# New order keys for every stage of a hybrid diffusion step on one NeuronCore

## The chip, the cores and the metric

The kernel runs on one core of one Trainium2 chip. The metric is the device time of one execution in microseconds (us). Before the change it is 1241.89 us, the median of three runs (1240.9 to 1245.12).

The engines are called by their names in the profile: PE is TensorE (matmuls; PEld is its weight load), DVE is VectorE, ACT is ScalarE, POOL is GpSimd, and SP is SyncE, which here only issues DMAs.

## The reference

One inference step of a backbone with two layers, on 256 context tokens and 1024 latent tokens of width 1024. The first layer is a gated linear attention (GLA) in both directions, the second a softmax attention with 8 query heads and 2 key heads. Each layer normalises its input, modulates it by a conditioning vector, runs its mixer, multiplies the result by a SiLU gate, projects it and adds it to the input. Cut to what matters:

```
for l in range(2):
    mod_p, mod_s = silu(c_ctx) @ w_ada[l] + b_ada[l], silu(c) @ w_ada[l] + b_ada[l]
    hp = rms_norm(xp, g[l]) * (1 + sc_p) + sh_p          # context tokens
    hs = rms_norm(xs, g[l]) * (1 + sc_s) + sh_s          # latent tokens
    if l == 0:                                            # GLA, 4 heads, chunks of 64
        q, k, v, gate = split(h @ w_in)
        decay = log_sigmoid((h @ wa1[d]) @ wa2[d] + ba[d]) / 16
        o = scan_forward(q, k, v, decay) + scan_backward(q, k, v, decay)
        out = (rms_norm(o) * silu(gate)) @ w_out
    else:                                                 # attention
        q, k = rope(rms_norm(q)), rope(rms_norm(k))       # rope on latent tokens alone
        out = (softmax(q k^T / sqrt(128)) v * silu(gate)) @ w_out
    x = x + gt * out
```

The outputs are both token streams, the final scan states of the context, and the keys and values of the context.

## The kernel before

Tokens come in ten tiles of 128 (two of context, eight latent). Every matmul of a projection is done in three parts of half precision: an operand is scaled by a power of two and split into a high and a low part (names ending in hi and lo, or h and l), and PE adds hi x hi, hi x lo and lo x hi (line 247). Making the low part is an operation of DVE with two inputs in SBUF, such as L1382, L309, L330 or L566. Transposes of half-precision tiles are DMAs that SP issues (L1383 for the softmax, L1055 for the rows of the first output projection).

The stages, with the times at which they run in the profile:

- Start (to about 84 us): weights of the modulation are loaded and multiplied, then the tokens are normalised (L535 to L542), transposed by PE (L548) and modulated. In one form of a modulation ACT makes the high part and DVE the full value (L561, L562), in the other ACT makes the full value and POOL copies the high part (L564, L565); DVE makes the low part (L566). Between the groups of tokens the small weights of the decay (the "rank") are split (L601 to L616) and its scales are worked out (L623 to L635).
- GLA layer (84 to about 480 us): head by head, tile by tile, a slot each. In a slot run the decay (L733 to L748), the decayed queries and keys (L758 to L768), the part within a chunk (intra, L781 to L793), the scan's outer products and states (L805 to L834; POOL does L830), the local part, the combination of both directions (L865 to L872), values and gates (L714, L718), the SiLU (L351 to L362) and the gated output (L879, L881), which SP stores in HBM (L882).
- Between the layers (480 to about 700 us): a fifth round over the tiles finishes the last head while the first output projection starts; rows are loaded again, split (out_prep, L1049 to L1055), projected with the residual (L1019 to L1030), modulated for the second layer (L508 to L520), and the first keys and queries are made (L1161 to L1207; POOL does the rotation L1172 and the square roots L238).
- Attention (700 to about 1147 us): ten steps of two query tiles and four heads. In each, scores (L1344) go to PSUM, DVE takes their maximum (L1347), ACT the exponential (L1352). A second piece, rest, normalises them: the high part by POOL for the first tile (L1379) or by ACT for the second (L1381), the low part by DVE (L1382), then the transposing DMA. The values of two heads back are multiplied by the transposed weights (L247, PT and vh), gated (L1407) and stored through POOL's queue (L1408). Key tiles of the context are written out through POOL's queue too (L1293, L1296). In the last step the rows of the first output tiles are loaded and prepared, and two pieces of the output (z.out, L1558 to L1562) and the last values (z.val) end it.
- Output (1147 us to the end): the second output projection, tile by tile (y, L247), with no order keys of its own.

The order of the instructions on each engine is fixed when the program is built. The framework keeps a running number that rises by one with each traced instruction, and its scheduler plays the program through a timeline and gives each engine, whenever it is free, the ready instruction with the lowest number. A step's number can be shifted:

```
def later(self, name, i=""):
    n = LATER.get(f"{name}{i}", LATER.get(name, 0))
    self.tc.cur_priority += n
    yield
    self.tc.cur_priority -= n
```

A negative entry of the table LATER lets the step go ahead of as many instructions, a positive one puts it behind them, among what is ready. A second argument picks one place: "a9.s1.3" is the second score of the fourth head in the last attention step, where "a9.s1" holds for the others. An explicit issue_after still holds an instruction behind another one on its engine. In attention, the names are a0 for the first two heads, a9 for the last step and a for the rest; s0 and s1 are the scores of the two tiles, q and qr the next query, val the values, key a key tile, gate the gates, rest the normalisation. In the GLA layer, gated, silu, A, ks, u, o, combine and the like are the parts of a slot, with a 9 for the fifth round; wo2, wo3, eres and emod belong to the weights and the early tiles of the first output projection. Names with x. belong to the stage between the layers, and those with s. to the start: s.rk is the rank's weights and scales, s.n1 and s.n2 the normalising of the second and third group of tokens, s.v the first value weights, s.q0 and s.q1 the first queries and keys.

## Time and profile before

| | value |
|---|---|
| median of three runs | 1241.89 us |
| the three runs | 1240.9, 1241.89, 1245.12 us |
| span of the profiled execution | 1240.9 us |
| instructions | 22365 |
| PE busy | 96% of the span |
| DVE busy | 76% |
| ACT busy | 55% |
| POOL busy | 26% |

The page gives, for the profiled execution, only its span, from the first to the last instruction; no time of its own is given beside it. A busy engine is one that has an instruction under way. Matmuls overlap: one of 256 columns is shown for 273 ns, though the next follows 109 ns later. PEclk is the share of full clock that PE was granted. A wait is put down to the operation that ended it, and a line may be that of a helper that many steps share, so a group is told apart by its tile names.

### The profile page before, as it was taken

The page shows a single profiled execution, that of the slowest core. Times are in us where ns is not written, and L with a number is a line of the kernel's source. Part 1 is how long each engine was busy: PE and PEld are TensorE (multiplying, and loading weights), DVE is VectorE, ACT ScalarE, POOL GpSimd, SP SyncE. Part 2 cuts the span into 40 slices and gives each one's busy share as a digit, 9 for nine tenths or more (in the row PEclk, how much of TensorE's full clock was granted, in tenths as well). Part 3 has the DMA queues.
Part 4 walks back from the last instruction along what each step waited for, and adds up shares of the span by engine and source line. Part 5 has one row for each costly group of instructions (what it writes and reads, how often), then busy time and mean ns, then how long its engine had stood idle before and what let it go on. Part 6 is the DMA issues. An engine that isn't in the chain of part 4 may idle for free. (4 is left out here: it accounts for less than half of the span.)

```text
span 1240.9 us, 22365 instructions
## 1 busy us (share of the span) xinstructions
PE 1190.7 (96%) x7990; PEld 778.3 (63%) x7990; DVE 944.9 (76%) x2177; ACT 687.0 (55%) x1694; POOL 320.5 (26%) x566
## 2 busy tenths in 40 slices
PE   5799999999999999799999999999999999989998
PEld 3467765655556566667776666776767666666444
DVE  4787779887888789976875787877767587786653
ACT  2565556665666657742333576666767676664110
POOL 0132122323321143311212443431322343311000
PEclk9999999999999999999999999999999999999999
DMA  9511566456555544489978787777958666979432
GB/s 378 196 69 73 196 202 228 127 185 203 175 191 164 189 132 161 112 186 307 204 174 203 178 163 138 132 145 133 199 124 161 124 118 132 205 139 246 158 137 85
DMA packets 318496, 210.14 MB, mean 169 GB/s; under 512 B 257158, under 2 KB 294702, under 8 KB 310064
## 3 DMA queue, kind: packets, MB, share of 16 engines
q1 hardware_dynamic: 311232, 191.18, 60.1%
q10 hardware_dynamic: 4688, 10.57, 2.2%
q0 software_dynamic: 2464, 6.95, 2.0%
q8 instruction: 63, 1.03, 0.3%
q14 instruction: 49, 0.40, 0.1%
HBM read 108.35 MB, written 38.96 MB: 119 GB/s over the span
## 5 line engine op out<-in xcount | busy, mean ns | idle before, releaser
L247 PEld LDWEIGHTS <-hT_hi 128*128 128x128 f16 x1920 | 187.6, 98 | 122.0 <-issue 5.6
L247 PE MATMUL mm<-whi,hT_hi 128*128 128x512 f16 (+1 forms) x576 | 200.2, 348 | 3.5 <-ACT gx L718 3.0
L247 PE MATMUL mm<-whi,hT_lo 128*128 128x512 f16 (+1 forms) x576 | 200.4, 348 | 0.0
L247 PE MATMUL mm<-wlo,hT_hi 128*128 128x512 f16 (+1 forms) x560 | 194.3, 347 | 0.7 <-DVE wlo L309 0.7
L247 PEld LDWEIGHTS <-whi 128*128 128x128 f16 x1232 | 120.3, 98 | 62.1 <-issue 2.2
L1344 PE MATMUL S<-kT,wst 128*128 128x512 f16 (+1 forms) x624 | 142.1, 341 | 4.1 <-ACT p L1352 4.0
L247 PE MATMUL mm<-hT_hi,whi 128*128 128x256 f16 (+1 forms) x480 | 141.1, 294 | 2.0 <-ACT gx L1392 2.0
L247 PE MATMUL mm<-hT_hi,wlo 128*128 128x256 f16 (+1 forms) x480 | 141.1, 294 | 0.0
L247 PE MATMUL mm<-hT_lo,whi 128*128 128x256 f16 (+1 forms) x480 | 141.1, 294 | 0.0
L1382 DVE SCALAR_TENSOR_TENSOR phl<-p,srec,phl 128x1280 f16<-128x1280 f32 (+1 forms) x79 | 105.3, 1332 | 40.6 <-ACT phl L1381 26.9
L247 PEld LDWEIGHTS <-hT_lo 128*128 128x128 f16 x960 | 94.1, 98 | 61.8 <-issue 1.1
L247 PE MATMUL mm<-PT,vh 128*128 128x256 f16 x672 | 114.6, 273 | 8.1 <-DMA PT<-phl 7.8
L1347 DVE TENSOR_REDUCE smx<-S 128x1 f32<-128x1280 f32 (+1 forms) x80 | 101.3, 1271 | 27.0 <-PE S L1344 26.9
L1352 ACT ACTIVATE p<-S,snb,acol 128x1280 f32<-128x1280 f32 (+1 forms) x80 | 99.1, 1239 | 12.5 <-DVE phl L1382 7.0
L1344 PEld LDWEIGHTS <-wst 128*128 128x128 f16 x624 | 61.4, 98 | 55.7 <-issue 6.9
L247 PE MATMUL mm<-PT,vl 128*128 128x256 f16 x336 | 91.6, 273 | 0.0
L1379 POOL TENSOR_SCALAR phl<-p,srec 128x1280 f16<-128x1280 f32 (+1 forms) x40 | 53.1, 1327 | 105.0 <-DVE srec L1370 57.1
L247 PEld LDWEIGHTS <-wlo 128*128 128x128 f16 x616 | 60.2, 98 | 29.2
L247 PEld LDWEIGHTS <-vh 128*128 128x128 f16 x672 | 65.1, 98 | 18.3 <-DMA PT<-phl 7.2
L1172 POOL TENSOR_TENSOR rope<-hx,ropet 128x64 f32<-128x64 f32 x160 | 51.2, 350 | 81.3 <-ACT hx L1308 63.8
L270 DVE TENSOR_REDUCE wmx<-wst 128x1 f32<-128x512 f32 x104 | 65.1, 677 | 3.5 <-DMA wst<-in_att_w 2.0
L238 POOL TENSOR_TENSOR hrs<-hrsa,mhalf 128x2 f32<-128x2 f32 x50 | 38.7, 775 | 106.8 <-DVE hrsa L236 106.5
(383 smaller groups left out, 2684.9 us busy)
## 6 DMA issues: line engine op xcount, KB each, us to landing
wada<-in_w_ada SPq DMA_DIRECT2D x16, 1024.0 KB, 5.4
wst<-in_att_w SPq DMA_DIRECT2D x14, 1024.0 KB, 5.3
wst<-in_gla_w_in SPq DMA_DIRECT2D x12, 1024.0 KB, 5.5
og_d<-og POOLq DMA_DIRECT2D x40, 128.0 KB, 2.8
wst<-og_d SPq DMA_DIRECT2D x5, 1024.0 KB, 6.0
og_d<-gx SPq DMA_DIRECT2D x37, 128.0 KB, 2.1
xr<-x_d SPq DMA_DIRECT2D x9, 512.0 KB, 3.3
out<-xr ACTq DMA_DIRECT2D x17, 256.0 KB, 2.0
```

Of the source, the lines that this page charges most:

```text
L238: nc.gpsimd.tensor_tensor(r, a, self.mhalf[:, 0:w], ALU.pow)
L247: self.pe = self.nc.tensor.matmul(out, a, b, start=k == 0 and j == 0, stop=k == n - 1 and j == 2).ins
L270: nc.vector.tensor_reduce(mx[:, j : j + 1], st[:, 2 * j : 2 * j + 2, :], AX.XY, ALU.max, apply_absolute_value=True)
L1172: nc.gpsimd.tensor_tensor(tv[:, h, :, w, :], xv[:, h, :, 1 - w, :], sn[:, :, w, :], ALU.mult)
L1344: nc.tensor.matmul(S[:, a : a + n], x, y, start=m == 0, stop=m == 2)
L1347: last = nc.vector.tensor_reduce(mx, S, AX.X, ALU.max).ins
L1352: nc.scalar.activation(p, S, AF.Exp, scale=self.sexp, bias=nb, accum_out=den)
L1379: nc.gpsimd.tensor_scalar(hi, p, r, 2.0 ** 14, ALU.mult, ALU.mult)
L1382: nc.vector.scalar_tensor_tensor(lo, p, r2, hi, ALU.mult, ALU.subtract)
```

## The change

The table LATER keeps its 93 names; 73 of the values are set anew, 38 lower and 35 higher, by a median of 55. Nothing else in the program changes: the same instructions run on the same engines with the same operands. The entries that moved by 100 or more, and some others:

```diff
-    "A": -110,            +    "A": -375,
-    "ks": -90,            +    "ks": 10,
-    "gated": 50,          +    "gated": -20,
-    "silu": -150,         +    "silu": -395,
-    "combine9": 70,       +    "combine9": 280,
-    "eres": 110,          +    "eres": 45,
-    "wo2": 30,            +    "wo2": 185,
-    "wo3": 245,           +    "wo3": 180,
-    "x.prep": -150,       +    "x.prep": 20,
-    "x.mod": -60,         +    "x.mod": -200,
-    "x.kset": -30,        +    "x.kset": 170,
-    "x.key8": 150,        +    "x.key8": -55,
-    "s.rk": 70,           +    "s.rk": -135,
-    "s.n1": -100,         +    "s.n1": 0,
-    "s.n2": -55,          +    "s.n2": -490,
-    "s.q1": 60,           +    "s.q1": 185,
-    "s.s0": -140,         +    "s.s0": 45,
-    "s.r1": 115,          +    "s.r1": 300,
-    "s.v": 400,           +    "s.v": 580,
-    "a0.qr": 15,          +    "a0.qr": 145,
-    "a0.gate": 65,        +    "a0.gate": 130,
-    "a0.s1": 390,         +    "a0.s1": 340,
-    "a.rest.0": 100,      +    "a.rest.0": -35,
-    "a.s0.1": -15,        +    "a.s0.1": -55,
-    "a.s1.0": 55,         +    "a.s1.0": -30,
-    "a9.s1": -160,        +    "a9.s1": -60,
-    "a9.val.1": -5,       +    "a9.val.1": -105,
-    "a9.val.3": -80,      +    "a9.val.3": -265,
-    "a9.q.2": 30,         +    "a9.q.2": -120,
-    "a9.gate.2": 85,      +    "a9.gate.2": 255,
-    "a9.s1.3": -150,      +    "a9.s1.3": 185,
-    "z.val": 35,          +    "z.val": 205,
-    "z.val.0": -100,      +    "z.val.0": 55,
-    "z.val.1": 165,       +    "z.val.1": -25,
```

The old value stands on the left of each line and the new one on the right.

## The prediction

> **What bounds the kernel now.** I read the page's busy row first, then a table of windows cut where the stages change, then who TensorE (PE) waits for.

> ```profile
> span 1240.9 us, 22365 instructions
> PE 1190.7 (96%) x7990; PEld 778.3 (63%) x7990; DVE 944.9 (76%) x2177; ACT 687.0 (55%) x1694; POOL 320.5 (26%) x566
> ```

> ```profile
> core 0: us, PE busy (x) PEld busy (x) DVE busy (x) ACT busy (x) POOL busy (x), PEclk, DMA share, GB/s
> 0.00:38.00 38.00, 21.27 (x202) 13.43 (x203) 16.51 (x46) 9.67 (x18) 2.95 (x8) 1.00 0.95 365
> 38.00:84.00 46.00, 39.17 (x241) 20.42 (x240) 39.63 (x86) 30.17 (x50) 9.92 (x15) 1.00 0.29 111
> 84.00:480.00 396.00, 395.70 (x2468) 244.90 (x2467) 328.78 (x891) 243.74 (x636) 113.36 (x207) 1.00 0.52 168
> 480.00:560.00 80.00, 71.97 (x513) 52.95 (x512) 68.53 (x193) 47.85 (x121) 20.93 (x34) 0.98 0.63 169
> 560.00:700.00 140.00, 140.00 (x1039) 101.40 (x1037) 103.58 (x224) 50.92 (x134) 33.34 (x73) 1.00 0.89 216
> 700.00:745.00 45.00, 40.65 (x290) 28.60 (x289) 34.36 (x66) 30.78 (x73) 17.95 (x28) 0.96 0.79 167
> 745.00:1080.00 335.00, 330.00 (x2360) 230.23 (x2359) 254.08 (x497) 229.41 (x593) 111.84 (x191) 1.00 0.73 145
> 1080.00:1147.00 67.00, 61.77 (x450) 43.39 (x448) 51.41 (x88) 37.93 (x68) 10.20 (x11) 1.00 0.89 194
> 1147.00:1240.90 93.90, 90.14 (x444) 43.03 (x442) 48.03 (x94) 6.56 (x6) 0.00 (x0) 1.00 0.37 129
> ```

> PE sets the time. Its work is the same under any order, so only its 50.2 us of idle time (1240.9 less 1190.7) can move. Length less PE busy gives the idle time of each stage: 16.7 before 38 us and 3.8 after 1147, which no key reaches (the weights are still loading; the last stage has no keys), and 6.8, 0.3, 8.0, 0, 4.4, 5.0 and 5.2 in between. So 29.7 us are within reach. VectorE (DVE) is never full: 328.8 of 396 us in the first layer.

> ```profile
> PE mm L247 <- DMA PT<-phl: 7.8, 6, 3.3
> PE S L1344 <- ACT p L1352: 4.0, 6, 2.3
> PE mm L247 <- ACT gx L718: 3.0, 1, 3.0
> PE mm L247 <- ACT gx L1392: 2.0, 1, 2.0
> PE z L548 <- DVE x L542: 1.8, 1, 1.8
> PE cs L548 <- DVE h L562: 1.4, 1, 1.4
> PE z L865 <- POOL Sc L830: 1.1, 2, 0.9
> PE mm L686 <- POOL hT_hi L565: 1.1, 2, 0.8
> PE z L205 <- DVE wm L290: 0.7, 1, 0.7
> PE U L865 <- POOL Sc L830: 0.6, 1, 0.6
> PE o L865 <- POOL Sc L830: 0.4, 1, 0.4
> ```

> The columns are total us, times and longest us. The waits are few and have different owners; no single one is the bound.

> **The change, part by part.** No instruction is added or removed. 73 numbers change, so the terms are stalls, not instructions.

> *The overlap itself.* Operations of DVE with two SBUF inputs do get longer beside GpSimd (POOL):

> ```profile
> L354 DVE SCALAR_TENSOR_TENSOR ls<-gx,ls x80: 406/418/1473, 179.1 to 1130.6; 128x256 f32<-128x256 f32 x80
> L354 DVE SCALAR_TENSOR_TENSOR ls<-gx,ls 128x256 f32<-128x256 f32 x80 | 40.6, 508 | 5.0 <-ACT ls L353 4.9
> L830 POOL TENSOR_SCALAR Sa<-Wa,eb,eb x32: 547/695/1416, 97.4 to 495.8; 128x256 f32<-128x256 f32 x32
> L1382 DVE SCALAR_TENSOR_TENSOR phl<-p,srec,phl x79: 470/1540/1605, 705.9 to 1125.4; 128x1280 f16<-128x1280 f32 x63, 128x256 f16<-128x256 f32 x16
> 729.43 1.33 POOL L1379 TENSOR_SCALAR phl<-p,srec 128x1280 f16<-128x1280 f32 x1
> 729.59 1.45 DVE L362 TENSOR_TENSOR gx<-gx,ls 128x256 f32<-128x256 f32 x1
> ```

> L354 takes 406 ns at its shortest and 508 on average: 80 times 102 ns is 8.2 us of stretching over the whole run, with a worst case of 1473. POOL's L830 goes from 547 up to 1416. In the last pair DVE starts at 729.59, POOL's 1.33 us end at 730.76, and DVE ends at 731.04: it seems to do its work only behind POOL. But the large L1382 never grows (1605 at most against 1540), and DVE has idle time to absorb the rest. [...]

> What of the stretching ends on PE? At most the waits that end in an operation open to it: 1.4 (L562), 1.1 (L565) and 1.1 + 0.6 + 0.4 (L830), 4.6 us in all. At the least, nothing. I take half, 2.3 us gained, since overlaps only become rarer.

> *Between the layers (480 to 560).* The keys of gated (50 to -20), silu (-150 to -395), combine9 (+210), eres (-65) and wo2/wo3 (+155, -65) change.

> ```profile
> 499.05 0.47 ACT L718 ACTIVATE gx<-mm,inv_g 128x256 f32<-128x256 f32 x1 [3.28 <-DMA og_d<-gx]
> DMA to landing us min/median/max: 1.7/2.1/5.5
> 499.40:502.80 3.40, 3.23 (x16) 2.23 (x16) 1.73 (x4) 3.34 (x8) 0.00 (x0) 0.50 0.00 0
> 731.50:734.90 3.40, 3.31 (x10) 1.43 (x10) 3.40 (x6) 0.75 (x3) 1.21 (x3) 0.50 0.38 72
> ```

> Here ScalarE (ACT) waits for a buffer of gx that a store (L882, the landing row) has not left: the slowest of 37 stores took 5.5 us where the median is 2.1. PE idles 3.0 us for it and 0.7 just before (wait for L290), and then runs 3.4 us at clock 0.50 (PEclk), which loses another 1.7: 5.4 us in all. A gated step is one DVE operation and this store on SP's queue; put 70 places earlier, the store can pass the loads it shares the DMAs with. The bounds are 5.4 gained and nothing; I take half, 2.7. If the loads pass it again instead, the price is the same stall once more.

> *Second layer's start (700 to 745).* a0.qr (+130), a0.gate (+65), a0.s1 (-50) and x.key8 (-205) move.

> ```profile
> 710.84 0.47 ACT L1287 ACTIVATE hx<-mm,inv_a 128x256 f32<-128x256 f32 x1 [5.50 <-DMA out<-hx]
> ```

> ACT's wait for an output store on POOL's queue ends in PE's 2.0 us (gx L1392). The later 2.3 (the longest for p L1352) is followed by the second window at clock 0.50, so the bound is 2.0 + 2.3 + 1.7 = 6.0 gained, or nothing. The store stays where it is, behind the same key tile; I take a quarter, 1.5.

> *Second layer's body.* a.rest.0 (100 to -35), a.s1.0 (-85) and a.s0.1 (-40) put the first half's normalisation (POOL, DVE and a transposing DMA on SP) earlier; SP's other transposes queue behind it. PE's remaining idle there is 5.0 + 5.2 us, mostly the 7.8 for PT. Bounds: 10 gained or nothing; I take 2.

> *Start (38 to 84).* s.rk (70 to -135) puts the rank's weights ahead of normalising the second group (s.n1, +100).

> ```profile
> 52.49 2.74 DVE L542 TENSOR_SCALAR x<-x,nt_r 128x1024 f32<-128x1024 f32 x4
> 55.14 0.16 DVE L218 TENSOR_SCALAR p2s<-p2e 128x2 int32<-128x2 int32 x1
> 58.82 0.15 DVE L635 TENSOR_SCALAR ninv_z<-inv_z 128x1 f32<-128x1 f32 x1
> ```

> DVE does the rank work from 55.14 to 58.97, 3.8 us behind L542's. In front of it, the transposes that PE waits 1.8 us for come up to 3.8 later; the rank's matmuls fill part of that. DVE's total before the next modulation is the same, so I take nothing; bounds 1.8 gained and 3.8 lost.

> *New stalls.* 73 moved keys in an order that leaves PE almost no slack will open holes elsewhere. The trace cannot show them; bounds are nothing and the largest present ones again (3.0 to 5.4); I take 3.0.

> **Sum:** -2.3 - 2.7 - 1.5 - 2.0 + 3.0 = -5.5 us, so the profiled 1240.9 becomes 1235.4. The page gives the span alone, which lies 1.0 below the median of the three runs (1241.89); with that 1.0, 1236.4.

> **Rivals.** *No change.* The overlaps fall, or do not fall at all because a key decides only between operations that are ready together, and in both cases PE was covered. For it: 0.3 us idle in the first layer in spite of the stretched operations. Against it: the 29.7 us elsewhere depend on order. Time 1241.9.

> *Slower: the last softmax.* a9.s1.3 goes from -150 to 185, the largest step of all, so the last scores may be placed behind the two output pieces (z.out).

> ```profile
> 1134.39 6.17 DMA wst<-og_d
> 1143.67 15.97 PE y L247 x74
> 1145.78 2.48 DVE L1542 SCALAR_TENSOR_TENSOR wlo<-wst,p2s,whi 128x1024 f16<-128x1024 f32 x2 [0.89 <-ACT whi L1541]
> ```

> Behind these scores hang their transposes and, on the same SP queue, the next row's load (1134.39), whose preparation ends at 1148.3. A matmul of y takes 15.97/74 = 0.216 us, so the two pieces, 2 x 24 matmuls, are 10.4 us, and the next row would be ready at 1158.7. PE has the 48 matmuls of the tile in hand until 1143.67 + 10.4 = 1154.1: it would wait 4.6 us, and 1.7 more for the clock. With nothing gained elsewhere that is 1241.9 + 6.3 = 1248.2. It decides once the shift is over 5.8 us. Against it: while both buffers of the bank for the pieces are taken, the scores still slip in.

> *Slower: the start.* The 3.8 us above in full, nothing gained elsewhere: 1245.7.

> The half clock behind a stall is in the trace twice. [...]

> **How the numbers follow.** Three runs can tell about 0.3%, 3.7 us, from no change. Forecast (gain of a few us): 0.50; no change: 0.27; last softmax: 0.13; start: 0.10. So faster 0.50, same 0.27, slower 0.23. The forecast's own range is 1227 to 1239: all the bounds gained without new stalls would be far more, but I count on no more than some 15 of the 33.1 us (29.7 and two half clocks). The overall range takes in the slower cases up to 1248, with about 1 in 10 left out on each side.

> **What would show it.** The mean of L354 nearer 418, and L830 nearer 695; no ACT wait of 3 us for og_d near 499; PE idle in 480:560 under 8.0 and in 700:745 under 4.4; no hole behind 1143. The prediction is wrong if the stretching shrinks while PE's idle stays at 50, or if a single wait over 3 us stands where none was.

## The result, and the profile after

| | before | after |
|---|---|---|
| median of 22 runs of each, taken together | 1245.26 us | 1243.0 us |
| lowest and highest | 1240.9, 1248.94 us | 1239.85, 1246.86 us |
| ratio after/before | | 0.998, 95% interval 0.9971 to 0.9988 |
| span of the profiled execution | 1240.9 us | 1238.7 us |

The change gains 0.2%, about 2.5 us. That is real (the interval excludes 1) and smaller than the 0.3% that the text of the prediction took as its bound. In the table of windows, whose columns and cuts are those shown of before, the idle time of PE is the length less the second number:

```profile
38.00:84.00 46.00, 40.60 (x239) 21.61 (x238) 38.20 (x82) 30.06 (x51) 10.59 (x17) 0.96 0.30 112
84.00:480.00 396.00, 395.11 (x2460) 244.06 (x2458) 325.64 (x890) 241.70 (x633) 112.36 (x206) 1.00 0.52 167
480.00:560.00 80.00, 73.03 (x524) 53.95 (x523) 72.02 (x199) 48.98 (x123) 21.48 (x34) 0.98 0.63 167
700.00:745.00 45.00, 42.59 (x302) 29.26 (x300) 34.73 (x66) 31.37 (x72) 17.90 (x28) 1.00 0.91 184
745.00:1080.00 335.00, 329.09 (x2370) 231.18 (x2368) 254.18 (x499) 229.81 (x597) 112.21 (x192) 1.00 0.72 146
1080.00:1147.00 67.00, 60.42 (x431) 41.76 (x430) 50.82 (x84) 35.44 (x61) 9.88 (x11) 1.00 0.86 186
```

Idle falls from 6.8 to 5.4 at the start, from 8.0 to 7.0 between the layers and from 4.4 to 2.4 in 700:745. It rises from 0.3 to 0.9, from 5.0 to 5.9 and from 5.2 to 6.6 elsewhere. In sum the 29.7 us that the keys can reach became 28.2. In 700:745 the clock is 1.00 where it was 0.96. Who PE waits for, in the view of the waits:

```profile
PE S L1344 <- ACT p L1352: 6.5, 7, 2.1
PE mm L247 <- DMA PT<-phl: 5.6, 6, 2.6
PE mm L247 <- ACT gx L718: 2.7, 1, 2.7
PE mm L205 <- DVE wm L1538: 2.0, 1, 2.0
PE mm L647 <- ACT wa1h L607: 1.8, 1, 1.8
PE z L865 <- POOL Sc L830: 1.2, 2, 1.0
```

The wait for gx L1392 (2.0) is gone and the one for gx L718, near 499, stands. Two of 2.0 (wm L1538) and 1.8 (wa1h) are new. The operations that the change is named for, in the views of their lines:

```profile
L354 DVE SCALAR_TENSOR_TENSOR ls<-gx,ls 128x256 f32<-128x256 f32 x80 | 39.4, 493 | 5.2 <-ACT ls L353 5.2
L830 POOL TENSOR_SCALAR Sa<-Wa,eb,eb x32: 548/583/1417, 97.3 to 496.0; 128x256 f32<-128x256 f32 x32
```

L354 takes 493 ns on average instead of 508, which is 1.2 us in the whole run. I also added up, over all POOL operations of each trace, the time that they lie beside DVE operations with two SBUF inputs: 158.2 us before, 160.8 after. (The issuing of DMAs on POOL is left out; which small operations are taken in shifts these sums by about 1 us.) The overlap did not fall.

What did change is the queue of ACT near 711. First two rows of before, around the one that the prediction showed (L1287, waiting 5.50 us until 710.84 for the store out<-hx), then after:

```profile
704.84 0.51 ACT L1206 ACTIVATE xhl<-hx,asc 128x256 f16<-128x256 f32 x1
...
712.85 1.41 ACT L1352 ACTIVATE p<-S,snb,acol 128x1280 f32<-128x1280 f32 x1
```

```profile
708.03 0.29 ACT L1349 ACTIVATE snb<-smx,acol 128x1 f32<-128x1 f32 x1 [3.31 <-DVE smx L1347]
708.35 1.36 ACT L1381 ACTIVATE phl<-p,srec 128x1280 f16<-128x1280 f32 x1
709.62 1.40 ACT L1352 ACTIVATE p<-S,snb,acol 128x1280 f32<-128x1280 f32 x1
...
712.90 0.47 ACT L1287 ACTIVATE hx<-mm,inv_a 128x256 f32<-128x256 f32 x1 [1.43 <-DMA out<-hx]
```

The store lands no earlier. But before, the exponential stood behind the instruction that waits for it: ACT started nothing between 704.84 and 710.84, and the exponential came at 712.85. After, the exponential comes first, at 709.62, and only L1287 itself waits.

### The profile page after: what moved, and what is told of

The parts are those of the page before. It is cut to its first block, busy times and chain, and to the rows that moved or that the text cites. A ratio compares the mean times of both kernels' runs of the same rounds, so it can differ in the third digit from the quotient of the medians.

```text
span 1238.7 us, 22382 instructions
## 1 busy us (share of the span) xinstructions
PE 1190.6 (96%) x7990; PEld 779.1 (63%) x7990; DVE 941.7 (76%) x2177; ACT 684.6 (55%) x1694; POOL 323.7 (26%) x566
## 5 line engine op out<-in xcount | busy, mean ns | idle before, releaser
L247 PEld LDWEIGHTS <-hT_hi 128*128 128x128 f16 x1920 | 187.6, 98 | 119.9 <-issue 3.8
L247 PE MATMUL mm<-whi,hT_hi 128*128 128x512 f16 (+1 forms) x576 | 200.1, 348 | 3.1 <-ACT gx L718 2.7
L247 PE MATMUL mm<-whi,hT_lo 128*128 128x512 f16 (+1 forms) x576 | 200.2, 347 | 0.0
L247 PE MATMUL mm<-wlo,hT_hi 128*128 128x512 f16 (+1 forms) x560 | 194.2, 347 | 0.7 <-DVE wlo L309 0.7
L247 PEld LDWEIGHTS <-whi 128*128 128x128 f16 x1232 | 120.2, 98 | 60.3 <-issue 0.9
L1344 PE MATMUL S<-kT,wst 128*128 128x512 f16 (+1 forms) x624 | 142.1, 338 | 6.5 <-ACT p L1352 6.5
L247 PE MATMUL mm<-hT_hi,whi 128*128 128x256 f16 (+1 forms) x480 | 141.0, 294 | 0.6 <-DVE og L1407 0.6
L247 PE MATMUL mm<-hT_lo,whi 128*128 128x256 f16 (+1 forms) x480 | 141.0, 294 | 0.0
L247 PE MATMUL mm<-hT_hi,wlo 128*128 128x256 f16 (+1 forms) x480 | 141.0, 294 | 0.0
L1382 DVE SCALAR_TENSOR_TENSOR phl<-p,srec,phl 128x1280 f16<-128x1280 f32 (+1 forms) x79 | 105.5, 1335 | 45.7 <-ACT phl L1381 28.4
L247 PEld LDWEIGHTS <-hT_lo 128*128 128x128 f16 x960 | 94.2, 98 | 61.3 <-issue 0.9
L247 PE MATMUL mm<-PT,vh 128*128 128x256 f16 x672 | 114.8, 273 | 5.8 <-DMA PT<-phl 5.6
L1352 ACT ACTIVATE p<-S,snb,acol 128x1280 f32<-128x1280 f32 (+1 forms) x80 | 99.0, 1238 | 8.9 <-DVE phl L1382 3.8
L1344 PEld LDWEIGHTS <-wst 128*128 128x128 f16 x624 | 61.0, 98 | 57.0 <-issue 7.7
L247 PE MATMUL mm<-PT,vl 128*128 128x256 f16 x336 | 91.6, 273 | 0.0
L1379 POOL TENSOR_SCALAR phl<-p,srec 128x1280 f16<-128x1280 f32 (+1 forms) x40 | 53.7, 1342 | 104.6 <-DVE srec L1370 57.8
L247 PEld LDWEIGHTS <-wlo 128*128 128x128 f16 x616 | 60.2, 98 | 29.4
L247 PEld LDWEIGHTS <-vh 128*128 128x128 f16 x672 | 65.2, 98 | 16.0 <-DMA PT<-phl 4.4
L1172 POOL TENSOR_TENSOR rope<-hx,ropet 128x64 f32<-128x64 f32 x160 | 53.9, 367 | 76.2 <-ACT hx L1308 61.9
L238 POOL TENSOR_TENSOR hrs<-hrsa,mhalf 128x2 f32<-128x2 f32 x50 | 40.1, 803 | 102.8 <-DVE hrsa L236 84.9
```

What stands on the lines that cost most here:

```text
L238: nc.gpsimd.tensor_tensor(r, a, self.mhalf[:, 0:w], ALU.pow)
L247: self.pe = self.nc.tensor.matmul(out, a, b, start=k == 0 and j == 0, stop=k == n - 1 and j == 2).ins
L1172: nc.gpsimd.tensor_tensor(tv[:, h, :, w, :], xv[:, h, :, 1 - w, :], sn[:, :, w, :], ALU.mult)
L1344: nc.tensor.matmul(S[:, a : a + n], x, y, start=m == 0, stop=m == 2)
L1352: nc.scalar.activation(p, S, AF.Exp, scale=self.sexp, bias=nb, accum_out=den)
L1379: nc.gpsimd.tensor_scalar(hi, p, r, 2.0 ** 14, ALU.mult, ALU.mult)
```

## Experiments

Every run is given as its ratio to the kernel before on the same chip with the 95% interval, and with a profile of its own. Theory A: the time is the sum of PE's local stalls, with the half-clock windows that the longer ones bring. Theory C: the overlap of GpSimd with two-input VectorE operations sets it.

**The change in parts.** Four kernels. After with the old entries of the last step and the output, and before with the new entries of one part:

```diff
 e1: after,  a9.* and z.* (22) old       e2: before, x.*, a0.*, a.* (20) new
 e3: before, s.* (11) new                e4: before, first layer (20) new
```

> The kernel after, with the 22 changed entries of the last attention step and of the output pieces (a9 and z) put back to their old values. In the list of instructions of each engine nothing then changes place against the kernel after: these entries are without effect, so the rival of the last softmax could not happen. Theory A (the time is the sum of local stalls of PE, each made or removed by the order near it): the ratio to the kernel before is that of the kernel after, 0.998, and the 2.2 us that the kernel after seemed to lose between 1098 and 1147 in its profile were an accident of one execution; its profile shows by how much the stages of one and the same program differ from run to run, up to some 2 us. Rival B (the loss at the end is real and comes from the keys): faster than the kernel after by 2.2 us, ratio 0.9962.

> The kernel before, with the 20 changed entries of x, a0 and a alone set anew. Theory A: the second layer's start (700 to 745) gains what it gained in the kernel after, 3.2 to 4 us, nothing changes before 480, and the whole is faster by about 3.2 us, ratio 0.9974; the half-clock window at 731 is gone and ACT's wait of 5.5 us for the store of hx is shorter. Theory C (what decides is how long two-input operations of VectorE and GpSimd lie on each other): the total of these overlaps must fall well below the 158.2 us of the kernel before for it to be faster, and it is no faster if they don't. Theory N (what differs between the two profiles is mostly the accident of one execution): ratio within 0.999 to 1.001.

> The kernel before, with the 11 changed entries of the start (s) alone set anew. Theory A: the start gained 1.4 us ahead of the first place where the entries act and lost 0.8 us behind it, so the entries themselves cost 0.8 us: ratio 1.0006, with a half-clock window near 52 that the kernel before does not show. Rival of the prediction (the rank's work of 3.8 us pushes the transposes out): 1.003. Theory N: within 0.999 to 1.001, window or not.

> The kernel before, with the 20 changed entries of the first layer and of its fifth round alone set anew. Theory A: 0.8 us lost in the first layer (a stall for kt at 221) and 0.8 us gained near 555, the stall of 2.7 to 3.0 us at 499 stays: ratio 1.000, within 0.0007. The prediction's term of -2.7 us between the layers would give 0.9978. Theory C: no gain unless the overlaps fall well below 158.2 us.

Measured: 0.9985 (0.997 to 1.0), 0.999 (0.9974 to 1.0006), 1.0001 (0.9982 to 1.002), 1.003 (1.0006 to 1.0053). The first is the program of after once more, and so a measure of chance: its profiled execution has a span of 1245.9 us, 7.2 more than that of after, at a clock of 0.991 instead of 0.997. So the stage differences of one pair of profiles, the 2.2 us "lost" at the end among them, say little. The average over runs says more: the 12 runs of e1 lose 5.9 us of their span to half clock (span times one less the granted clock), the 35 runs of before on the same chip 7.3, and the rest of the span is 1235.8 against 1236.7 us. Roughly, the gain is thus partly fewer windows at half clock and partly less waiting, as Theory A has it. The start (e3) does nothing that can be measured, and the window near 52 that Theory A expected is not in its profile. The profiles of e9 and e15, with the old entries of the start, do have one (at 52.9 and 53.3), so that window does not come from these entries. e2 gains in the place that Theory A names, though its time is nearer to no change than forecast, and its interval leaves room for Theory N. Its overlap is 168.6 us, the largest of these kernels, and it is not slower for it, which speaks against Theory C. The first layer's entries alone cost 0.3%, where Theory A had expected nothing.

**Which entry.** The gain of e2 divided:

```diff
 e9: before, x.* (7) new                 e10: before, a0.* and a.* (13) new
 e11: before, first layer and x.* (27) new    e8: after, first layer (20) old
 e15: before, "x.key8": 150 -> -55       e16: after, "x.key8": -55 -> 150
```

> The kernel before, with the 7 changed entries of x (the stage between the layers) alone set anew. Three kernels with the new x, a0 and a entries show 1.1 and 1.3 to 1.9 us of idle PE between 700 and 745 and no window at half clock there; three with the old ones show 3.6 to 4.3 us and one or two windows. Theory A with the gain in the entries of x: this picture of the new kind, ratio as of the run with x, a0 and a together, 0.999 or lower. Rival (it lies in a0 and a): the old picture, a stall of 2 us or more at 713 to 715, ratio 1.000.

> The kernel before, with the 13 changed entries of a0 and a alone set anew. Theory A with the gain in the entries of x: the old picture between 700 and 745 (3.6 us or more idle), ratio 1.000. Rival (the gain lies in a0 and a): 2.4 to 2.9 us idle there, ratio 0.999 or lower.

> The kernel before, with the 20 changed entries of the first layer and the 7 of x set anew together. If the entries of the first layer cost 0.3% by themselves only because the load of the key weights then came late at 573 under the old entries of x: no stall at 573 and a ratio of 0.998 to 0.999, as of the kernel after. If the parts add up: 1.002.

> The kernel after, with the 20 changed entries of the first layer and its fifth round put back to their old values. If the parts of the change add up (these entries alone gave 1.003): 0.995, faster than both kernels. Rival (these entries cost something only together with the old entries of x, where the load of the key weights came late at 573): 0.998, as in the kernel after, and no stall at 573.

> The kernel before with one entry set anew, x.key8 from 150 to -55. In the order of ACT it alone puts the exponential of the second scores ahead of the activation that waits for the store of hx near 711. Theory A: it brings the whole gain, 0.998; ACT's wait for the store 1 to 2 us instead of 5.5 to 7.1, PE's idle time between 700 and 745 about 2.1 to 2.9 us instead of 3.6 to 4.4, no window at half clock there. Rival (the gain needs the other entries too): 1.000.

> The kernel after with this one entry put back, x.key8 at 150. Theory A: the gain is gone, 1.000 (the other 72 entries together give nothing that can be measured); ACT's wait for the store near 711 is 5.5 us or more again. Rival: 0.998.

Measured: e9 0.9982 (0.9964 to 1.0001), e10 1.0001 (0.9986 to 1.0016), e11 1.0001 (0.9981 to 1.0021), e8 0.9996 (0.9982 to 1.0009), e15 0.9987 (0.9974 to 1.0), e16 0.9995 (0.9984 to 1.0006). The window 700:745 of e15, and its ACT instruction that waits for the store in the timeline:

```profile
700.00:745.00 45.00, 42.47 (x305) 29.73 (x304) 35.61 (x69) 32.70 (x79) 18.18 (x28) 1.00 0.87 178
```

```profile
714.59 0.47 ACT L1287 ACTIVATE hx<-mm,inv_a 128x256 f32<-128x256 f32 x1 [1.54 <-DMA out<-hx]
```

The same two of e16:

```profile
700.00:745.00 45.00, 41.42 (x294) 29.24 (x292) 35.06 (x66) 30.55 (x73) 17.50 (x28) 0.96 0.78 167
```

```profile
712.16 0.47 ACT L1287 ACTIVATE hx<-mm,inv_a 128x256 f32<-128x256 f32 x1 [6.95 <-DMA out<-hx]
```

One entry turns the one picture into the other. (It moves more than this exchange: against before, 72 places in ACT's order and 93 in VectorE's are different in e15.) Of the twelve kernels that differ in entries alone, the five with the old x.key8 (before, e3, e4, e10, e16) wait 5.5 to 7.2 us on ACT, leave PE 3.9 us idle there on average and have one window at half clock on average (none to two). The seven with the new one wait 1.1 to 2.1 us, leave 2.7 us idle and have no window. That is 1.2 + 1 x 1.7 = 2.9 us, a little more than the gain of after. By the times alone the entry is worth less: 1.6 us in e15 against before, and 1.9 in e16 against after, and the intervals allow anything from nothing to the whole gain. The place is shown by the profiles; that it is the whole gain is not shown. The parts do not add up: the first layer's entries cost 0.3% alone (with a stall of 1.45 us for the key weights at 573 that no other of the twelve has), e11 lies between its two expectations, and e8 missed both of its own, since after without these entries is rather slower than faster. Why is not settled.

**Taking the waits away by buffers.**

```diff
 e5, after:  "gx" of the first layer, bufs=3 -> bufs=4 (and "s0" shares the buffer of "mod")
 e6, before: context key tiles in a buffer of their own, "hxc", instead of "hx4"
```

> The kernel after, with a fourth buffer for gx in the first layer (the room for it comes from sharing the small buffer s0 with another of the same size). Theory A (the time is the sum of PE's stalls, and of the half-clock windows that the longer ones bring): ACT's wait for the store of gated output near 499, which stands in all six profiles with 2.2 to 3.9 us of PE, goes, and with it the half-clock window behind it, 1.7 us or more; so 4 us faster than the kernel after, ratio to the kernel before 0.995. Rival (the store is late whatever the buffers, and the next wait for it takes the place): ratio 0.998 as in the kernel after, with a stall of over 2 us between 490 and 515.

> The kernel before with all its keys, and a buffer of their own for the key tiles of the context (hxc), so that ACT no longer waits for the store of hx near 711. Theory A: this wait is what the keys of x, a0 and a removed; without it PE's stall of 2.0 to 3.7 us at 713 is gone, the windows at half clock behind 713 and 731 become rarer, and the whole gains about 2 to 3.4 us, ratio 0.9975. Rival (the wait for p L1352 behind it takes its place): ratio 1.000, with 4 us or more of idle PE still between 700 and 745.

Measured: e5 1.0083 (1.0066 to 1.01), e6 1.0036 (1.0019 to 1.0053): both theories' numbers missed. In e5 PE still waits 2.1 us for gx L718, so a fourth buffer does not cure the late store, as the rival said; the loss comes with new stalls, 2.68 us for the shared s0 among them, so that the run does not say more. In e6 the ACT wait is gone, and this is what comes instead, in the waits and the windows:

```profile
PE mm L247 <- DMA PT<-phl: 13.2, 8, 3.5
```

```profile
700.00:745.00 45.00, 36.44 (x263) 25.35 (x262) 32.90 (x62) 30.92 (x79) 18.01 (x31) 1.00 0.72 153
```

PE is idle for 8.6 us there. So taking the wait away gains nothing by itself. That the gain comes from the exponential going ahead of the waiting instruction fits e15 and e16; no run changes that alone.

**More GpSimd work beside VectorE.** Operations that nothing uses, added to the kernel after. In e7, e12 and e13 they are 128 x 128, in e14 one element per partition:

```diff
 e7, 4 in each SiLU of both layers (320); e12, 6 at each gate of attention (240):
+        nc.gpsimd.tensor_scalar(dummy, ident, x[:, 0:1], 1.0, ALU.mult, ALU.mult)
 e13, 3 behind each row maximum (240):
+        nc.gpsimd.tensor_scalar(dummy, ident, mx, 1.0, ALU.mult, ALU.mult)
 e14, 3 at the same place (240):
+        nc.gpsimd.tensor_tensor(dummy, mx, mhalf[:, 0:1], ALU.pow)
```

> The kernel after, with 320 more operations of GpSimd, 128 x 128 each, four behind every SiLU's input, that read two small tiles and write a spare one; nothing uses what they make. By the shortest POOL operations of the trace they add some 60 to 100 us to POOL's 324, and about half of it lies beside two-input operations of VectorE, as half of POOL's present work does: the overlap goes from 161 to about 200 us. Theory A (PE is covered, the overlap costs nothing): ratio within 0.997 to 1.000, as in the kernel after, though L354, L362 and L330 take longer. Theory C (the overlap sets the time): the stretching of both engines grows by about a quarter, some 14 us; if half of it reaches PE the kernel is 7 us slower than the kernel after, ratio 1.004.

> The kernel after, with 240 more operations of GpSimd in the attention stage alone, where PE waits for none of POOL's operations directly; 128 x 128 each, about 0.5 us, six behind each gate's input; nothing uses what they make, and the order of everything else is the same but for a few dozen of 22,000 instructions. In the run with 320 such operations in both layers the 8 us that were lost lay between 480 and 560, where PE waits for the states that POOL scales, and 0.9 us in 745 to 1080. Theory A (overlap that PE does not wait for costs nothing): VectorE's busy time grows by 8 us or more in 745 to 1080, PE's idle time there by no more than 1 or 2, ratio 0.998 to 0.9995. Theory C (the overlap sets the time): the overlap in this stage doubles, and the loss is of the order of the added stretching, 8 us or more, ratio 1.004.

> The kernel after, again with 240 more operations of GpSimd in attention (128 x 128, 0.37 us where nothing lies beside them; nothing uses what they make), but three behind each row maximum instead of six behind each gate: there POOL has to wait for the exponential of 1.4 us in any case, so that they should be done before the next operation that something waits for. Theory A (overlap that PE does not wait for costs nothing, and the run with six in a row lost its 8 us to operations queued behind them on POOL): ratio 0.998 to 1.000, PE's idle time in 745 to 1080 no more than 2 us above the 5.9 of the kernel after. Theory C (the overlap itself sets the time): a loss as in the run with six in a row, 1.004 or more.

> The same as the run before it in this call, with operations of one element per partition (a power, 0.55 us, longer than those of 128 x 128) in place of those of 128 x 128: POOL is occupied for longer, but hardly any data moves. Theory A (occupation of POOL's queue is what costs): as slow as the run before it or slower by 1 to 3 us, with the same kind of waits (PT, srec). If what costs is the data that both engines move: faster than it, ratio as of the kernel after, 0.998.

Measured: e7 1.0047 (1.0029 to 1.0065), e12 1.0063 (1.0041 to 1.0086), e13 1.0122 (1.0107 to 1.0137), e14 1.0178 (1.0164 to 1.0192). All four miss Theory A's numbers: the added work does cost. But Theory C's mechanism is not what the profiles show either. In e7, the windows of the two layers and of the stage between, and one of its waits (its lines behind L364 are one higher than in after):

```profile
84.00:480.00 396.00, 394.80 (x2456) 243.52 (x2455) 329.15 (x889) 242.17 (x634) 163.00 (x321) 1.00 0.52 166
480.00:560.00 80.00, 70.30 (x481) 51.05 (x479) 67.45 (x190) 45.27 (x117) 39.32 (x74) 0.94 0.57 150
745.00:1080.00 335.00, 328.04 (x2341) 228.28 (x2340) 262.20 (x495) 228.92 (x592) 177.89 (x317) 1.00 0.71 142
```

```profile
PE o L866 <- POOL Sc L831: 2.7, 1, 2.7
```

In 84:480 POOL has 50.6 us more to do and PE idles 0.3 us more; in 745:1080 it is 65.7 us more, VectorE is busy 8.0 us longer, and PE idles 1.1 us more. The loss is in 480:560, with 9.7 us idle and clock 0.94, where PE waits for what POOL itself makes, and 2.3 us in 560:700, where after has none. In e12 it is attention that loses, with VectorE no longer busy than in after:

```profile
745.00:1080.00 335.00, 323.16 (x2289) 224.79 (x2288) 249.26 (x486) 224.39 (x584) 197.87 (x375) 0.99 0.69 138
```

PE idles 11.8 us there instead of 5.9. For what it waits, the groups of instructions show, with the idle time of the engine in front of them: first two of after, then of e13 and of e14 (where L1379 and L1382 are L1380 and L1383), each with the row of PE's wait for the transposes.

```profile
L1379 POOL TENSOR_SCALAR phl<-p,srec 128x1280 f16<-128x1280 f32 x32 | 48.9, 1528 | 82.7 <-DVE srec L1370 52.1 <-DMA PT<-phl 29.1 <-ACT ls L352 1.4
L1382 DVE SCALAR_TENSOR_TENSOR phl<-p,srec,phl 128x1280 f16<-128x1280 f32 x63 | 97.4, 1546 | 37.2 <-ACT phl L1381 26.7 <-POOL phl L1379 10.4
```

```profile
L354 DVE SCALAR_TENSOR_TENSOR ls<-gx,ls 128x256 f32<-128x256 f32 x80 | 38.4, 480 | 2.0 <-ACT ls L353 1.9
L1380 POOL TENSOR_SCALAR phl<-p,srec 128x1280 f16<-128x1280 f32 x32 | 45.7, 1428 | 6.2 <-DMA PT<-phl 3.6 <-DVE srec L1371 2.4
```

```profile
PE mm L247 <- DMA PT<-phl: 20.8, 11, 2.8
```

```profile
L354 DVE SCALAR_TENSOR_TENSOR ls<-gx,ls 128x256 f32<-128x256 f32 x80 | 34.8, 435 | 5.9 <-ACT ls L353 5.9
L1383 DVE SCALAR_TENSOR_TENSOR phl<-p,srec,phl 128x1280 f16<-128x1280 f32 x63 | 97.5, 1548 | 63.4 <-ACT phl L1382 37.8 <-POOL phl L1380 25.3
```

```profile
PE mm L247 <- DMA PT<-phl: 17.7, 11, 2.9
```

In after POOL stands ready 82.7 us before the high parts; in e13 that is 6.2. It now comes to them late, VectorE's low part waits for POOL 25.3 us instead of 10.4 (e14), the transposes follow, and PE waits for PT 20.8 and 17.7 us instead of 5.6. These rows do not explain e12: there the same two sums are 56.4 and 9.1 us, and PE still waits 10.7 us for PT. The slowest kernel of all, e14, has the least stretched L354 (435 ns; in before it is 416 where no POOL operation lies beside it; its L362 is longer, 470 against 442) and 936.9 us of VectorE against 941.7 in after. So in e13 and e14 POOL's place in a chain costs; a stretched VectorE operation by itself was not seen to. The kernels that differ in entries alone agree: their overlap runs from 152.1 us (e4, the slowest) over 159.1 (e15) and 161.9 (e10, no change) to 168.6 (e2) and 168.2 us (e9, among the fastest). No run took the overlap away, so what it costs altogether stays open.

**Less on POOL's queue.**

```diff
-        nc.gpsimd.dma_start(self.og2_d[c, :, h, :], og)
+        nc.sync.dma_start(...)   # e17       nc.scalar.dma_start(...)   # e18
```

> The kernel after, with the 40 stores of the attention's output issued by SP in place of POOL, which takes POOL's 23.4 us of issuing (0.584 us each) off its queue. Theory Q (what POOL's queue is occupied with is what counts in attention: 168.5 us of idle work on it cost some 22 us, 139.6 us some 15, so about 0.11 to 0.13 us each): 2.5 to 3 us faster than the kernel after, ratio 0.996. Rival (SP's transposes then queue behind stores that wait for VectorE, and PE waits longer for PT): 0.998 or above, with more than the 5.6 us that PE waits for PT in the kernel after.

> The same with ACT issuing the 40 stores. Theory Q: as in the run with SP, 0.996. Rival (ACT's exponentials then stand behind a store that waits for VectorE, as they stood behind the wait for hx near 711): above 0.998, with more than the 6.5 us that PE waits for p in the kernel after.

Measured: e17 0.9977 (0.9961 to 0.9993), e18 0.9968 (0.9954 to 0.9982). Both beat the kernel before. e17 is where after is, so Theory Q missed it; its waits for PT are 5.9 us, hardly more than 5.6, so the rival's reason is not seen either. e18 has the lowest ratio of all, but its interval overlaps that of after, so that a gain of 0.1% over after is possible and not shown. In e18 PE waits for PT 4.0 us instead of 5.6, and for p 6.6 as against 6.5. In both, POOL is idle about twice as long before L1379 as in after (159.2 and 156.3 us against 82.7), and at least in e17 PE gains nothing from it: loading POOL's queue costs, but emptying it does not pay back at the same rate.

## Why the prediction was wrong, point by point

The direction was right, the size was not: -5.5 us forecast, about -2.5 measured. The direction is partly luck, since three of the four gains in the sum did not come and the loss hardly came either. Of the distance between 1236.4 and 1243.0, 3.4 us are the base: the three runs known then had a median of 1241.89, all 22 have 1245.26. The rest is the sum.

- **The step that failed first: 73 moved numbers were taken for 73 moved steps.** Put back in the kernel after, one at a time or all together, 52 of the 73 entries change the place of no instruction on any engine, so that 21 make the whole difference. Among the 52 are gated9, silu, wo3, a0.qr, a0.gate, a0.s1, a.rest.0, a.s1.0, s.n1 and all of a9 and z, on which terms of the sum and a rival were built. A key decides only between operations that are ready together; the prediction says so under its rival "no change" and does not use it in the sum.
- **Overlap, -2.3.** Failed: the overlap did not fall (158.2 to 160.8 us), and L354 was stretched least in the slowest run of all. The prediction's own sign of being wrong came near here: L354's mean fell to 493 ns while PE's idle time went only from 50.2 to 48.1 us. Nor does it say much that L1382 never grows: of the 17 of the large ones that start in before while POOL is running, 16 start beside the issuing of a DMA, and the one beside an operation on data (L1172) is the longest, at 1605 ns. The test "L830 nearer 695" was no test either: 695 is the median in that view; it is 583 after.
- **Between the layers, -2.7.** Failed: the wait near 499 stands in all twenty profiles with 1.7 to 4.1 us (in e7 split into two). Its half-clock window stands in after too. The entries of the first layer alone (e4), which hold all that this term names, made the kernel 0.3% slower. Half was taken without a reason from the profile why the store should land earlier.
- **Second layer's start, -1.5.** Right place, right stall, even the right entry (x.key8). The size is 2.9 us by the profiles and 1.6 to 1.9 by the times of e15 and e16, so that 1.5 came close, but by luck: a quarter was taken and no mechanism given. The prediction saw that the store stays where it is and concluded that little could change. But one can also move what stands behind the waiting instruction on ACT's queue, and that was worth a quarter to a half of the bound of 6.0.
- **Body, -2.0.** Failed: e10 gives 1.0001, and in after two of the three entries that the term names (a.rest.0 and a.s1.0) move nothing.
- **Start, 0.** Right (1.0001 in e3), within its bounds. The profile of after has 1.4 us less idle there and pays 1.7 us for the window at 51.9, which other kernels have under the old entries too.
- **New stalls, +3.0.** They hardly came: 1.8 for wa1h stands where 1.8 for x (L542) stood, 0.8 at 221 is not in the other profile of the same program, and the wait for wm L1538 is anything from 0 to 2.6 us in the twenty profiles, with old entries (2.6 in e3) as with new.
- **Rivals.** The last softmax could not happen at all, since a9.s1.3 moves nothing; nor was its step, 335, the largest of all, for s.n2 went 435 down. The start did not lose. "No change" came closest in size (by the bound of 0.3% the result is one of no change), for the reason named in it.

## What to carry to other kernels

Before costing a table of priorities, compare the programs: find out which entry changes which engine's order. Then look for an instruction that waits for a DMA at the head of its engine's queue, as L1287 did on ACT (before: nothing started between 704.84 and 710.84), and ask what ready work stands behind it. An engine that is busy for 26% of the time can still be on the chain, as POOL is here (with the work of e13 in its queue PE's wait for PT went from 5.6 to 20.8 us): count how long it stands ready before the operation that matters, not its share.

## What the runs showed of the hardware

```profile
495.95:499.36 3.41, 0.23 (x1) 0.11 (x2) 2.52 (x15) 0.31 (x1) 1.43 (x2) 1.00 0.39 141
499.36:502.78 3.42, 3.21 (x16) 2.21 (x16) 1.71 (x4) 3.36 (x8) 0.00 (x0) 0.50 0.00 0
...
728.06:731.47 3.41, 1.28 (x12) 0.99 (x11) 3.41 (x7) 2.91 (x9) 2.83 (x6) 1.00 0.82 159
731.47:734.88 3.41, 3.29 (x10) 1.41 (x10) 3.41 (x6) 0.76 (x3) 1.22 (x3) 0.50 0.39 74
...
1093.28:1096.70 3.42, 1.78 (x9) 0.78 (x8) 3.42 (x7) 0.52 (x3) 0.63 (x2) 1.00 1.09 223
1096.70:1100.11 3.41, 1.48 (x14) 1.34 (x15) 3.41 (x3) 2.95 (x4) 0.00 (x0) 1.00 0.74 141
```

A stall of 2.25 us, 2.13 of it within one cell (PE busy 1.28 of 3.41), is followed by half clock in the next. One of 3.29 us that lies across two cells (1.78 and 1.48 busy) is not. Counted over the twenty profiles behind 40 us, outside cells that are at half clock themselves: of 43 cells with more than 2.03 us idle 43 are followed by half clock, of 70 with 1.6 to 2.03 us 17, of 68 with 1.2 to 1.6 us none. In before and after alone it is 3 of 3, 1 of 6 (1.95 us idle from 48.48 in after) and none of 5. So here 2.13 us idle in one cell were enough, and 3.29 us over two were not. The grid lies 0.32 us earlier in after than in before (499.04 and 499.36), and the executions of one program did not pay the same number of windows: the profiled ones of after and of e1 have two and six before the last, at 1.7 us each (granted clock 0.997 and 0.991), and this is most of the 7.2 us between their spans. This was read from the traces; no run set a stall to a chosen length.

**Beside some POOL operations L354 was stretched, beside others not.** In before, L354 takes 416 ns on average where no POOL operation lies beside it (27 cases), 418 beside a power of L238 alone (8) and 751 beside L1379 alone (19, up to 1473); the pair at 729, L362 with 1.45 us beside L1379, is of the last kind. In e14, L354 takes 414 ns on average where a power of one element per partition is already running as it starts (14 cases) and 420 where none is (5); L362 413 (22 cases) and 420 (7). In e13, beside operations of 128 x 128, L354 goes from 416 to 452 and L362 from 415 to 481. The power itself takes 543 ns at its shortest in before (L238) and 702 on average in e14. The profile's times of POOL operations are rough, so which part of such an operation stretches the one beside it is not shown here.
